# A two-layer hybrid block on one core: seven products of quarters in the feed-forward layer, another order of experts, one weight slot fewer

## The chip, the cores and the metric

The kernel runs on one core of a Trainium2 chip. The metric is the device time of one execution in microseconds (us), lower is better. Engines are named as in the profile: PE (TensorE, matrix products), PEld (its weight loads), DVE (VectorE), ACT (ScalarE), POOL (GpSimd), SP (the queue that issues the transfers).

## The reference

256 tokens of a sequence and 256 tokens of a context, each of width 1024, pass through two layers. The first layer mixes with a gated recurrence and an attention, then applies a dense feed-forward layer to all 512 tokens; the second mixes with a long convolution and a latent attention, then applies eight experts, two of them per token, to the 256 tokens of the sequence. Cut to what the change touches:

```python
D_MODEL, D_FF, N_EXPERTS, TOP_K, D_FF_EXPERT = 1024, 2816, 8, 2, 3584

def swiglu(h, w1, w3, w2):                # all in float32
    return (jax.nn.silu(h @ w1) * (h @ w3)) @ w2

# first layer:  h is 512 x 1024, w1 and w3 are 1024 x 2816, w2 is 2816 x 1024
xl = xl + mod_l[5] * swiglu(modulate(rms_norm(xl, ...)), ffn_w1, ffn_w3, ffn_w2)     # and the same for the context
# second layer: each token goes through its two best experts, with the gates as weights
out = sum(gate * swiglu(t, moe_w1[e], moe_w3[e], moe_w2[e]))
```

## The kernel before, in words

**Products in two parts.** Every float32 matrix is held as a high part (rounded to the engine's fast float32 format, `fp32r`) and a low part (the rest). A product takes three matmuls: high by high, high by low and low by high (`mm3`, L576 to L579). For a weight block, ACT writes the high part (`Stream.split_to`, L260) and DVE the low part, the block minus its high part (`lows`, L273); in some stretches the low part is POOL's (`ws.low = P`).

**Weights.** A `Stream` keeps the list of all weight blocks in the order of their use. A block is 1 MB (128 partitions by 2048 floats). SP loads it into a raw tile, it is split into pairs of tiles `whi` and `wlo` (four of each, 1024 wide) and PE reads these. In the layers before the experts there are two raw tiles.

**The feed-forward layer** (L1093 to L1150). The 22 row tiles (128 wide) of the hidden layer are done in three parts of 8, 8 and 6 (`FFN_PARTS`). In a part, two tiles at a time, which this text calls a pair, PE multiplies a block of w1 (256 columns, eight tiles k of the width) and a block of w3 with the normed input, 48 matmuls of 512 tokens for each block. ACT takes the silu (L1120), DVE multiplies (L1124) and the result is split again (`hilo`, L555 to L557). Then four blocks of w2 finish the part. The first pair of the first part is special: its k loop follows the norm (`norm_pair`, L568: `xn` on DVE L564, `hhi` on ACT L565, `hlo` on DVE L566) and its order is fixed by hand. `tick` (L448) is one small matmul of the modulation vectors; ticks stand between the pairs and the blocks. The tiles `xn` form a ring of four.

**The experts.** Experts are ranked by load: ranks 1 and 2 have room for 128 tokens (full: float32 in two parts, split like above), the other six for 64 (small: plain float32, unsplit). `SEQ` (L345) is the order of the ranks. Each expert is 42 blocks of 1 MB. Blocks flow into a ring of slots (L1475 to L1515), filled in their order as the slots come free (`Stream.fill`, L222); in the last stretch there are 13: five of their own, two raw tiles, five places of buffers that are no longer used, and half of `xT`, the transposed input (L1873), which is free from the middle of the first expert on.

Of the kernel before, what the change touches and what calls it, by code (L numbers as in the profile page):

```python
# [10 lines left out]
F32 = mybir.dt.float32  # L11
# [127 lines left out]
def program(tc, a, out):  # L139
# [174 lines left out]
    for m0, mn in FFN_PARTS:  # L314
        for b in range(mn // 2):
            want(*colblk('ffn_w1', (m0 + 2 * b) * 128, 256))
            want(*colblk('ffn_w3', (m0 + 2 * b) * 128, 256))
        for c0 in range(0, 1024, 256):
            want(*colblk('ffn_w2', c0, 256, m0, m0 + mn))
# [24 lines left out]
    CAP = [64] + [128] * BIG + [64] * (7 - BIG)  # L344
    SEQ = [(x, CAP[x] == 64) for x in (0, 3, 1, 4, 2, 5, 6, 7)]  # L345
    which = {}
# [228 lines left out]

    def mm3(p, wh, wl, xh, xl, first, last):  # L576
        TE.matmul(p, wh, xh, start=first, stop=False)  # L577
        TE.matmul(p, wh, xl, start=False, stop=False)  # L578
        TE.matmul(p, wl, xh, start=False, stop=last)  # L579

# [472 lines left out]
    ap = fx.enter_context(tc.tile_pool(name="ap", bufs=8, reuse_waits="tile"))  # L1053
    mod_ring([(mq, "rm", 2)] * 2 + [(ap, "rm", 6)] * 6, 72)

# [35 lines left out]
    first = [take(0), take(0)]  # L1091
    h = []
    for m0, mn in FFN_PARTS:  # L1093
        act = []
        for b in range(mn // 2):
            if m0 + b == 0:
                p1, p3 = [bank(), bank()], bank2()
                h.append(norm_pair(pb, 0, 1, 0))
                for k in range(KD):
                    if k + 1 < KD:  # L1100
                        h.append(norm_pair(pb, 0, 1, k + 1))
                    for (bh, bl), pq in zip(first, (p1, (p3[:, 0, :], p3[:, 1, :]))):
                        for m in range(2):
                            c = slice(m * 128, m * 128 + 128)
                            mm3(pq[m], bh[:, k, c], bl[:, k, c], h[k][0], h[k][1], k == 0, k == KD - 1)
                ws.split_to(ws.pos[2])
                order.close()
            else:
                bh, bl = take()
                p1 = [bank(), bank()]  # L1110
                for m in range(2):
                    c = slice(m * 128, m * 128 + 128)
                    for k in range(KD):
                        mm3(p1[m], bh[:, k, c], bl[:, k, c], h[k][0], h[k][1], k == 0, k == KD - 1)
                bh, bl = take()
                p3 = bank2()
            for m in range(2):
                c = slice(m * 128, m * 128 + 128)
                s = ap.tile([128, T], F32, name=nm("fs"), tag="fs", bufs=2)
                A.activation(s, p1[m], AF.Silu)  # L1120
                if m0 + b:
                    for k in range(KD):
                        mm3(p3[:, m, :], bh[:, k, c], bl[:, k, c], h[k][0], h[k][1], k == 0, k == KD - 1)
                V.tensor_tensor(s, s, p3[:, m, :], op=OP.mult)  # L1124
                n = len(act) % 4
                if n == 0:
                    ah, al = wide("ah"), wide("al")
                hi, lo = ah[:, n, :], al[:, n, :]
                hilo(hi, lo, s)
                act.append((hi, lo))  # L1130
# [554 lines left out]
    def moe(st, units, slots, main):  # L1685
# [156 lines left out]
        for n in range(len(units) + 1):  # L1842
# [15 lines left out]
            if n:  # L1858
# [52 lines left out]
```

## Time and profile before

| | us |
|---|---|
| runs of before, median of 3 (lowest, highest) | 1726.57 (1723.56, 1729.68) |
| profiled execution, its own time | 1723.7 |
| its span, first to last instruction | 1721.7 |
| PE busy | 1617.6 (94% of the span) |
| DVE busy | 767.6 (45%) |
| ACT busy | 580.3 (34%) |
| POOL busy | 113.0 (7%) |
| bytes moved | 476.03 MB, mean 276 GB/s |

How to read it: the span divides into the first mixing (0 to about 290 us), the feed-forward layer (about 290 to 680), the second mixing (to about 840) and the experts (to the end). The busy share of an engine is a mean over these; what limits a stage is read from that stage. A busy PE is one with matmuls in flight: they are pipelined, so the time of one in the rows is longer than the distance from one start to the next, and it is the distance that counts. The time of DVE and POOL instructions runs from start to end, waiting for memory included.

### The profile page before, as it was taken

How to read it: one execution, taken by the hardware profiler on the slowest of the kernel's cores; microseconds unless marked ns; L12 is line 12 of the kernel's file. 1: busy time of each engine (PE TensorE's matmuls, PEld its weight loads, DVE VectorE, ACT ScalarE, POOL GpSimd, SP SyncE). 2: the span in 40 equal slices, each digit the busy share in tenths (PEclk: the TensorE clock that was granted, in tenths of full speed). 3: DMA queues.
4: the chain of work that ended last, by engine and by line, in shares of the span. 5: the costliest groups of instructions: out<-in, count | busy, mean ns of one | idle time of the engine just before them, and what ended most of it. 6: DMA issues, size and time to landing. Idle time of an engine off the chain costs nothing. (4 is left out here: it accounts for less than half of the span.)

```text
span 1721.7 us, 21415 instructions
## 1 busy us (share of the span) xinstructions
PE 1617.6 (94%) x8369; PEld 1025.8 (60%) x8369; DVE 767.6 (45%) x1214; ACT 580.3 (34%) x872; POOL 113.0 (7%) x81
## 2 busy tenths in 40 slices
PE   6898889999999999989999998999999999988886
PEld 2675666887777776776843434776446763423222
DVE  6679856334333326768630103884128852000001
ACT  3465743322222223554420103674136751000000
POOL 1433200000000000340000000000000000000000
PEclk9998999999999999999999999999999999999999
DMA  9534325223323333553799999999999989999997
GB/s 353 205 120 169 123 98 190 92 98 122 110 105 117 110 104 132 196 202 111 279 386 417 417 418 419 416 417 377 419 413 421 402 302 416 416 419 419 414 419 294
DMA packets 98989, 476.03 MB, mean 276 GB/s; under 512 B 8560, under 2 KB 34544, under 8 KB 53632
## 3 DMA queue, kind: packets, MB, share of 16 engines
q1 hardware_dynamic: 96256, 468.25, 69.3%
q0 software_dynamic: 1536, 5.28, 0.9%
q8 instruction: 68, 1.11, 0.3%
q10 hardware_dynamic: 1088, 1.05, 0.2%
q14 instruction: 41, 0.34, 0.1%
HBM read 471.40 MB, written 3.15 MB: 276 GB/s over the span
## 5 line engine op out<-in xcount | busy, mean ns | idle before, releaser
L273 DVE TENSOR_TENSOR wlo<-raw,whi 128x1024 fp32r<-128x1024 f32 (+2 forms) x240 | 282.1, 1209 | 201.4 <-ACT whi L260 193.9
L260 ACT ACTIVATE whi<-raw 128x1024 fp32r<-128x1024 f32 (+2 forms) x271 | 275.1, 1044 | 280.6 <-PE pm L578 115.7
L1736 PE MATMUL pm<-raw,xs 128*64 128x512 f32 (+1 forms) x1336 | 305.4, 551 | 23.2 <-DMA raw<-in_moe_w_dram 22.5
L1736 PEld LDWEIGHTS pm<-raw,xs 128*64 128x64 f32 x1336 | 103.7, 137 | 190.3 <-issue 138.0
L1855 DVE TENSOR_TENSOR es<-es,pm 128x512 f32<-128x512 f32 (+1 forms) x38 | 24.5, 644 | 339.6 <-PE pm L1736 328.5
L1736 PE MATMUL p<-raw,ats 128*64 128x512 f32 x616 | 152.2, 598 | 5.0 <-DMA raw<-in_moe_w_dram 4.3
L273 POOL TENSOR_TENSOR wlo<-raw,whi 128x1024 fp32r<-128x1024 f32 (+1 forms) x31 | 75.7, 2456 | 559.5 <-ACT k L1236 485.7
L1767 ACT ACTIVATE ats<-pm 128x512 f32<-128x512 f32 (+1 forms) x24 | 13.1, 544 | 285.1 <-PE p L1736 249.9
L577 PE MATMUL pm<-hhi,whi 128*128 128x512 f32 x240 | 96.4, 407 | 3.8 <-ACT hhi L565 3.8
L578 PE MATMUL pm<-hlo,whi 128*128 128x512 f32 x240 | 96.9, 404 | 1.0 <-DVE hlo L566 1.0
L1756 PE MATMUL pm<-wlo,xe 128*128 128x512 f32 x224 | 92.6, 414 | 4.0 <-DVE wlo L273 4.0
L579 PE MATMUL pm<-hhi,wlo 128*128 128x512 f32 x240 | 95.8, 400 | 0.0
L1736 PEld LDWEIGHTS p<-raw,ats 128*64 128x64 f32 x616 | 43.6, 136 | 86.8 <-issue 68.4
L1755 PE MATMUL pm<-whi,xe 128*128 128x512 f32 x224 | 88.0, 399 | 3.0 <-ACT whi L260 3.0
L577 PE MATMUL p<-hhi,whi 128*128 128x512 f32 x224 | 89.0, 398 | 1.3 <-ACT hhi L556 0.7
L578 PE MATMUL p<-hlo,whi 128*128 128x512 f32 x224 | 89.1, 398 | 0.0
L579 PE MATMUL p<-hhi,wlo 128*128 128x512 f32 x224 | 88.8, 396 | 0.0
L1848 ACT ACTIVATE es<-pm 128x512 f32<-128x512 f32 (+1 forms) x38 | 21.2, 559 | 156.2 <-PE pm L1736 150.7
L577 PE MATMUL pm<-ah,whi 128*128 128x512 f32 x176 | 70.2, 402 | 0.0
L458 PE MATMUL pm<-rm,sc 128*32 128x256 f32 x768 | 61.7, 408 | 8.8 <-DMA rm<-in_mod_w_dram 7.4
L578 PE MATMUL pm<-al,whi 128*128 128x512 f32 x176 | 69.6, 397 | 0.0
L579 PE MATMUL pm<-ah,wlo 128*128 128x512 f32 x176 | 69.0, 396 | 0.0
(454 smaller groups left out, 2678.6 us busy)
## 6 DMA issues: line engine op xcount, KB each, us to landing
raw<-in_moe_w_dram SPq DMA_DIRECT2D x300, 1024.0 KB, 15.2
rm<-in_mod_w_dram SPq DMA_DIRECT2D x96, 512.0 KB, 4.7
raw<-in_ffn_w_dram SPq DMA_DIRECT2D x30, 1024.0 KB, 4.8
xT<-in_moe_w_dram SPq DMA_DIRECT2D x24, 1024.0 KB, 18.4
raw<-in_ab_w_in_dram SPq DMA_DIRECT2D x7, 1024.0 KB, 6.6
raw<-in_cd_w_in_dram SPq DMA_DIRECT2D x6, 1024.0 KB, 6.5
whi<-in_moe_w_dram SPq DMA_DIRECT2D x12, 512.0 KB, 15.3
raw<-in_ab_w_out_dram SPq DMA_DIRECT2D x4, 1024.0 KB, 4.9
```

Source lines behind the costliest of these rows:

```text
L260: x = A.activation(h, c, AF.Copy)
L273: x = low.tensor_tensor(l, r, h.bitcast(F32), op=OP.subtract)
L458: TE.matmul(mst[2][32 * i:32 * i + 32, :256], sc[:, k, :], r[:, i * 256:(i + 1) * 256], start=k == 0, stop=k == 7)
L577: TE.matmul(p, wh, xh, start=first, stop=False)
L578: TE.matmul(p, wh, xl, start=False, stop=False)
L579: TE.matmul(p, wl, xh, start=False, stop=last)
L1736: TE.matmul(o if len(w.shape) == 2 else o.rearrange("p (a b) -> p a b", b=S), x, w, start=start, stop=stop)
L1755: TE.matmul(p, xh[:, k, :], bh[:, k, :], start=hf == 0 and k == 0, stop=False)
L1756: TE.matmul(p, xh[:, k, :], bl[:, k, :], start=False, stop=False)
L1767: A.activation(at[:, :n], p[:, :n * 128].rearrange("p (i s) -> p i s", i=n), AF.Copy)
L1848: A.activation(s[:, :w], p1[:, :w], AF.Silu)
L1855: V.tensor_tensor(s[:, :w], s[:, :w], p3[:, :w], op=OP.mult)
```

## The change

All blocks of w1 and w3 but the first pair's are computed by Strassen's scheme: the block is cut into four quarters (128 columns by 512 of the width), the input into four (512 of the width by 256 tokens), and seven products of sums of quarters replace eight products of quarters. `quarters` makes five sums of the input once: three into tiles of their own (products 1, 6, 7; adds on POOL), two in place of quarters that are no longer needed (3, 4; adds on DVE); each is split by ACT and DVE. `Sevens.ahead` makes the weight sums (POOL, for five of the seven) and splits each of the seven (ACT, DVE); `Sevens.block` runs the products (84 matmuls of 256 tokens for a block), and combines them: two copies on ACT, one add on POOL, five adds on DVE. The ring of modulation rows in the feed-forward pool shrinks (`RM`), the order of the experts changes in one place and the slot in `xT` is gone.

```diff
+    RM, SW = 2, 3
-    SEQ = [(x, CAP[x] == 64) for x in (0, 3, 1, 4, 2, 5, 6, 7)]
+    SEQ = [(x, CAP[x] == 64) for x in (0, 3, 1, 4, 5, 2, 6, 7)]
-    mod_ring([(mq, "rm", 2)] * 2 + [(ap, "rm", 6)] * 6, 72)
+    mod_ring([(mq, "rm", 2)] * 2 + [(ap, "rm", RM)] * RM, 72)
...
+    def quarters():
+        for q in (1, 6, 7):
+            sums_q[q] = [ap.tile([128, 4, S], F32R, name=f"h{q}_{t}", tag=f"h{q}{t}", bufs=1) for t in ("hi", "lo")]
+        for k in range(4):
+            x, y = h[k], h[k + 4]
+            for q, (u, cu), (v, cv), op, E in ((1, (x, U0), (y, U1), OP.add, P), (6, (x, U0), (x, U1), OP.add, P),
+                                               (3, (x, U1), (y, U1), OP.subtract, V), (7, (y, U0), (y, U1), OP.add, P),
+                                               (4, (y, U0), (x, U0), OP.subtract, V)):
+                z = nw.tile([128, S], F32, name=nm("xn"), tag="xn", bufs=4)
+                E.tensor_tensor(z, u[0][:, cu].bitcast(F32), v[0][:, cv].bitcast(F32), op=op)
+                E.tensor_tensor(z, z, u[1][:, cu].bitcast(F32), op=OP.add)
+                E.tensor_tensor(z, z, v[1][:, cv].bitcast(F32), op=op)
+                hi, lo = [x[:, k, :] for x in sums_q[q]] if q in sums_q else [x[:, cu] for x in u]
+                A.activation(hi, z, AF.Copy)
+                V.tensor_tensor(lo, z, hi.bitcast(F32), op=OP.subtract)
+    MS = [(5, OP.add, (0, 0), (0, 1)), (2, OP.add, (1, 0), (1, 1)), (1, OP.add, (0, 0), (1, 1)), (3, None, (0, 0), None),
+          (4, None, (1, 1), None), (6, OP.subtract, (1, 0), (0, 0)), (7, OP.subtract, (0, 1), (1, 1))]
...
+        def ahead(self, n):
+            while len(self.parts) < min(n, len(self.todo)):
...
+                if n0 % 2 == 0:
+                    self.t = [wp.tile([128, W // 2], F32R, name=nm(t), tag=t, bufs=2 * NH) for t in ("whi", "wlo")]
...
+                if op:
+                    z2 = ap.tile([128, 4, 128], F32, name=nm("sw"), tag="sw", bufs=SW)
+                    P.tensor_tensor(z2, z, self.r[:, 4 * y[1]:4 * y[1] + 4, 128 * y[0]:128 * y[0] + 128], op=op)
+                    z = z2
+                A.activation(hi, z, AF.Copy)
+                V.tensor_tensor(lo, z, hi.bitcast(F32), op=OP.subtract)
...
+        def block(self, j):
...
+            for i, (q, *_) in enumerate(MS):
+                n0 = 7 * j + i
+                self.ahead(n0 + 5)
...
+                for k in range(4):
+                    mm3(dest[q], hi[:, k, :], lo[:, k, :], *met(q, k), k == 0 and q not in (3, 4, 7), k == 3, q in (3, 4, 7))
+                if q == 5:
+                    A.activation(d, pX, AF.Copy)
+                if q == 2:
+                    A.activation(s2, pY, AF.Copy)
+                    P.tensor_tensor(d, d, s2, op=OP.add)
+                if q == 1:
+                    V.tensor_tensor(t, pZ, d, op=OP.subtract)
+                if q == 6:
+                    V.tensor_tensor(t, t, pW, op=OP.add)
+                    V.tensor_tensor(t, t, pX, op=OP.add)
+            V.tensor_tensor(e, pZ, d, op=OP.subtract)
+            V.tensor_tensor(e, e, pY, op=OP.add)
+            return [[e, pX], [pY, t]]
...
+                j = 2 * (b - (m0 == 0))
+                fs = [ap.tile([128, T], F32, name=nm("fs"), tag="fs", bufs=2) for _ in range(2)]
+                for m, x in enumerate(sevens.block(j)):
+                    for c, u in zip(x, (U0, U1)):
+                        A.activation(fs[m][:, u], c, AF.Silu)
+                for m, x in enumerate(sevens.block(j + 1)):
+                    for c, u in zip(x, (U0, U1)):
+                        V.tensor_tensor(fs[m][:, u], fs[m][:, u], c, op=OP.mult)
+                    activations(fs[m])
...
+            if b == 3 and m0 < 16:
+                sevens = Sevens(FFN_PARTS[m0 // 8 + 1][1])
+                sevens.ahead(4)
...
-                        ws.slots.insert(0, [lambda: xT[:, :, S:], -1, None])
-                        ws.fill()
```

What stands on the engines at the two places of which the prediction speaks:

POOL around the feed-forward layer, before: the last instructions of the first mixing (`hlo`, `u`, `hhi`) are followed at once by those of the second (`wlo` from `raw`); in the feed-forward layer POOL has none.

```order
L885 TENSOR_TENSOR hlo_1854<-u,hhi_1853 128x512
L885 TENSOR_TENSOR hlo_1887<-u,hhi_1886 128x512
L885 TENSOR_TENSOR hlo_1952<-u,hhi_1951 128x512
L273 TENSOR_TENSOR wlo_5169<-raw_5043,whi_5167 128x1024
L273 TENSOR_TENSOR wlo_5170<-raw_5043,whi_5168 128x1024
L273 TENSOR_TENSOR wlo_5260<-raw_5175,whi_5258 128x768
```

POOL at the start of the Strassen pairs, of the change: `sw` are weight sums from a raw block, `xn` the sums of the input's quarters (`hhi`, `hlo`).

```order
L1148 TENSOR_TENSOR sw_2900<-raw_2376 128x512
L1110 TENSOR_TENSOR xn_2679<-hhi_2478 128x256
L1111 TENSOR_TENSOR xn_2673<-xn_2673,hlo_2479 128x256
L1110 TENSOR_TENSOR xn_2691<-hhi_2554 128x256
L1111 TENSOR_TENSOR xn_2679<-xn_2679,hlo_2479 128x256
L1112 TENSOR_TENSOR xn_2673<-xn_2673,hlo_2555 128x256
L1111 TENSOR_TENSOR xn_2691<-xn_2691,hlo_2555 128x256
L1112 TENSOR_TENSOR xn_2679<-xn_2679,hlo_2479 128x256
L1112 TENSOR_TENSOR xn_2691<-xn_2691,hlo_2555 128x256
L1110 TENSOR_TENSOR xn_2703<-hhi_2488,hhi_2576 128x256
```

POOL now has 156 instructions between those two places: 100 weight sums, 36 adds for the input and 20 adds `dd`.

DVE in one pair of the first part, before: low parts of weight blocks (`wlo`, 1024 wide), products with w3's result (`fs`), low parts of the activations (`al`).

```order
L273 TENSOR_TENSOR wlo_2888<-raw_2759,whi_2886 128x1024
L273 TENSOR_TENSOR wlo_2889<-raw_2759,whi_2887 128x1024
L1124 TENSOR_TENSOR fs_2897<-fs_2897,p_508_2896 128x512
L557 TENSOR_TENSOR al_2925<-fs_2897,ah_2924 128x512
L273 TENSOR_TENSOR wlo_2965<-raw_2834,whi_2963 128x1024
L1124 TENSOR_TENSOR fs_2928<-fs_2928,p_508_2896 128x512
L273 TENSOR_TENSOR wlo_2966<-raw_2834,whi_2964 128x1024
L557 TENSOR_TENSOR al_2925<-fs_2928,ah_2924 128x512
```

DVE in the change, between the first and the second Strassen pair: `wlo` is now 512 wide and comes from a weight sum `sw` or from a raw block; `dd` are the combinations, with one input in PSUM (`pm`, `p`).

```order
L1151 TENSOR_TENSOR wlo_3146<-sw_3147,whi_3145 128x512
L1225 TENSOR_TENSOR fs_2818<-fs_2818,dd_2961 128x256
L1151 TENSOR_TENSOR wlo_3146<-sw_3166,whi_3145 128x512
L1225 TENSOR_TENSOR fs_2817<-fs_2817,dd_2962 128x256
L559 TENSOR_TENSOR al_2659<-fs_2818,ah_2658 128x512
L559 TENSOR_TENSOR al_2659<-fs_2817,ah_2658 128x512
L1151 TENSOR_TENSOR wlo_3183<-sw_3184,whi_3182 128x512
L1151 TENSOR_TENSOR wlo_3183<-sw_3200,whi_3182 128x512
L1176 TENSOR_TENSOR dd_3108<-pm_3104,dd_3106 128x256
L1178 TENSOR_TENSOR dd_3108<-dd_3108,pm_3105 128x256
```

Four low parts of 1024 in a pair have become fourteen of 512, and ten combinations have come in. On PE, all the ticks that stood between the pairs and the w2 blocks of the feed-forward layer stand in the first two Strassen pairs.

## Rows read from the trace of the kernel before

**Rows 1.** The page: the span and the number of instructions.

```profile
span 1721.7 us, 21415 instructions
```

**Rows 2.** Busy time by window: us, PE, PEld, DVE, ACT, POOL, PEclk, DMA, GB/s.

```profile
320.00:340.00 20.00, 20.00 (x88) 16.05 (x87) 4.15 (x5) 3.83 (x5) 0.00 (x0) 1.00 0.24 91
640.00:660.00 20.00, 20.00 (x92) 15.36 (x91) 9.88 (x20) 8.98 (x13) 0.00 (x0) 1.00 0.29 93
```

**Rows 3.** Timeline of PE in the feed-forward layer: start us, us, instruction.

```profile
316.80 0.39 PE L577 MATMUL pm<-hhi,whi 128*128 128x512 f32 x1
...
349.83 0.39 PE L577 MATMUL pm<-hhi,whi 128*128 128x512 f32 x1
...
353.34 0.40 PE L577 MATMUL p<-hhi,whi 128*128 128x512 f32 x1
...
668.69 0.64 PE L458 MATMUL pm<-rm,sc 128*32 128x256 f32 x8
669.26 0.50 PE L577 MATMUL pm<-ah,whi 128*128 128x512 f32 x1
...
677.56 0.39 PE L579 MATMUL pm<-ah,wlo 128*128 128x512 f32 x1
```

**Rows 4.** Timeline of PE in the second mixing, 256 tokens wide.

```profile
836.06 0.28 PE L577 MATMUL pm<-hl,whi 128*128 128x256 f32 x1
...
837.12 0.28 PE L577 MATMUL pm<-hl,whi 128*128 128x256 f32 x1
```

**Rows 5.** Timeline of POOL, 143 to 151 us.

```profile
144.31 1.29 POOL L882 TENSOR_TENSOR u<-u,gate 128x512 f32<-128x512 f32 x1 [2.02 <-DVE nr L507]
145.55 2.35 POOL L273 TENSOR_TENSOR wlo<-raw,whi 128x1024 fp32r<-128x1024 f32 x1
147.86 2.26 POOL L882 TENSOR_TENSOR u<-u,gate 128x512 f32<-128x512 f32 x1
```

**Rows 6.** Timeline of DVE in the same stretch and, last, at 157 us.

```profile
144.37 1.23 DVE L783 TENSOR_TENSOR t<-p,nr 128x1024 f32<-128x1024 f32 x1
145.63 3.36 DVE L785 TENSOR_TENSOR t<-t,row 128x1024 f32<-128x1024 f32 x1
149.02 1.25 DVE L793 TENSOR_TENSOR t<-t,rope 128x128 f32<-128x128 f32 x1
150.20 0.28 DVE L794 TENSOR_TENSOR t<-t,rope 128x128 f32<-128x128 f32 x1
...
157.03 1.22 DVE L785 TENSOR_TENSOR t<-t,row 128x1024 f32<-128x1024 f32 x1
```

**Rows 7.** Timeline of DVE at the start of the feed-forward layer.

```profile
290.44 0.48 DVE L566 SCALAR_TENSOR_TENSOR hlo<-xn,modc,hhi 128x256 fp32r<-128x256 f32 x1 [0.18 <-ACT hhi L565]
...
302.31 0.88 DVE L566 SCALAR_TENSOR_TENSOR hlo<-xn,modc,hhi 128x256 fp32r<-128x256 f32 x2 [0.18 <-ACT hhi L565]
...
319.03 1.29 DVE L557 TENSOR_TENSOR al<-fs,ah 128x512 fp32r<-128x512 f32 x2
```

**Rows 8.** Groups by line and shape: count, busy us, mean ns of one, idle before.

```profile
L557 DVE TENSOR_TENSOR al<-fs,ah 128x512 fp32r<-128x512 f32 x22 | 15.1, 689 | 7.2 <-ACT ah L556 7.1
```

**Rows 9.** Busy time by window among the experts, columns as in rows 2.

```profile
1100.00:1120.00 20.00, 20.00 (x86) 15.37 (x85) 17.24 (x17) 14.47 (x17) 0.00 (x0) 1.00 1.02 416
...
1180.00:1200.00 20.00, 20.00 (x90) 9.05 (x90) 3.77 (x4) 7.60 (x10) 0.00 (x0) 1.00 0.84 322
...
1360.00:1380.00 20.00, 20.00 (x89) 16.00 (x88) 16.48 (x16) 15.10 (x17) 0.00 (x0) 1.00 0.96 377
1380.00:1400.00 20.00, 20.00 (x100) 16.12 (x100) 16.97 (x16) 13.32 (x15) 0.00 (x0) 1.00 0.96 357
1400.00:1420.00 20.00, 20.00 (x92) 11.39 (x93) 6.53 (x8) 6.24 (x9) 0.00 (x0) 1.00 0.66 239
```

**Rows 10.** PE's waits, 1000:1080 then 1500:1600: us in total, times, longest.

```profile
PE pm L1736 <- DMA raw<-in_moe_w_dram: 1.0, 2, 0.6
...
PE pm L1736 <- DMA raw<-in_moe_w_dram: 7.7, 9, 1.4
```

**Rows 11.** The page's DMA issues: line, count, KB each, us to landing.

```profile
xT<-in_moe_w_dram SPq DMA_DIRECT2D x24, 1024.0 KB, 18.4
```

**Rows 12.** Busy time by window in the second mixing, columns as in rows 2.

```profile
680.00:700.00 20.00, 17.31 (x134) 12.88 (x127) 18.06 (x43) 9.05 (x19) 0.00 (x0) 0.83 0.26 82
```

More of the change, by code (lines that the diff above doesn't have):

```diff
@@ L315, in program @@
         for b in range(mn // 2):
-            want(*colblk('ffn_w1', (m0 + 2 * b) * 128, 256))
-            want(*colblk('ffn_w3', (m0 + 2 * b) * 128, 256))
+            for w in ('ffn_w1', 'ffn_w3'):
+                src, cols, _, shape = colblk(w, (m0 + 2 * b) * 128, 256)
+                want(src, cols, m0 + b == 0, shape)
         for c0 in range(0, 1024, 256):
@@ L574, in norm_pair, with mm3 @@
         return hi, lo
[L576 to L579, printed above, removed]
+    def mm3(p, wh, wl, xh, xl, first, last, more=False):
+        TE.matmul(p, wh, xh, start=first, stop=False, skip_group_check=more)
+        TE.matmul(p, wh, xl, start=False, stop=False, skip_group_check=more)
+        TE.matmul(p, wl, xh, start=False, stop=last, skip_group_check=more)
     def norm_full():
@@ L1092, in program @@
     h = []
+    U0, U1 = slice(0, S), slice(S, T)
+    sums_q = {}
+    def quarters():
[13 more added lines that the diff above has]
+                V.tensor_tensor(lo, z, hi.bitcast(F32), op=OP.subtract)
@@ L1093, in program, with activations @@
+    sevens = None
     for m0, mn in FFN_PARTS:
         act = []
+        def activations(s):
+            n = len(act) % 4
+            if n == 0:
+                whole[:] = wide("ah"), wide("al")
+            hi, lo = [x[:, n, :] for x in whole]
+            hilo(hi, lo, s)
+            act.append((hi, lo))
+        whole = []
         for b in range(mn // 2):
@@ L1105, in program @@
                             mm3(pq[m], bh[:, k, c], bl[:, k, c], h[k][0], h[k][1], k == 0, k == KD - 1)
-                ws.split_to(ws.pos[2])
                 order.close()
-            else:
[L1109 to L1130, printed above, removed]
+                for m in range(2):
+                    s = ap.tile([128, T], F32, name=nm("fs"), tag="fs", bufs=2)
+                    A.activation(s, p1[m], AF.Silu)
+                    V.tensor_tensor(s, s, p3[:, m, :], op=OP.mult)
+                    activations(s)
@@ new lines, in program @@
+                sevens = Sevens(mn - 2)
+                quarters()
+                sevens.ahead(4)
+            else:
+                j = 2 * (b - (m0 == 0))
[7 more added lines that the diff above has]
+                    activations(fs[m])
@@ L1131, in program @@
             tick()
         for b in range(4):
-            bh, bl = take()
+            bh, bl = take(0 if b == 3 and m0 < 16 else None)
+            if b == 3 and m0 < 16:
+                sevens = Sevens(FFN_PARTS[m0 // 8 + 1][1])
+                sevens.ahead(4)
             for m in range(2):
```

27 lines of the change are left out of this document (added).

## The prediction

> **What bounds the kernel now.** I read the span [rows 1], the busy times by window, and then the timeline of each engine where the change puts work. From 316.80 us, where the pair after the special first one begins, to 677.56 us the feed-forward layer runs on PE alone: PE is busy in all 20 us of a window, DVE in 4 to 10, POOL in none [rows 2]. Starts of 512-token matmuls lie 3.51 us apart over 15 of them, 0.234 us each [rows 3]. So a pair (two blocks of 48) takes 22.5 us. Ten such pairs are 225 us, the w2 blocks 22 x 8 x 3 matmuls or 123.6 us, together 348.6 of the 360.8 us; the remaining 12.2 us fit the ticks, 0.57 us each from one start to the next instruction [rows 3]. Every microsecond PE saves here reaches the end, since all later stages follow from this one, if another resource does not take its place.
>
> Among the experts the bound is the transfer of the weights, 416 GB/s [rows 9], but for three places where all slots are full and the queue waits: 322 GB/s after the first full expert, 377, 357 and 239 during and after the second.
>
> **PE's gain.** A 256-token matmul starts 1.06 us after the ninth before it, 0.118 us each [rows 4], so half the width costs half the time. A block becomes 84 x 0.118 = 9.9 us, a pair 19.8 us: 2.7 us saved, 27 us over ten pairs. That is the whole good of the scheme, and it needs PE to be fed at that pace.
>
> **What feeds it.** POOL's rows and DVE's have to be read together. At 145.55 us POOL starts a 1024-wide subtraction of two tiles in SBUF; DVE's L785, also two tiles in SBUF, starts at 145.63 and takes 3.36 us, where the same line takes 1.22 us at 157.03. It ends at 148.99. POOL's next instruction, 512 wide, takes 2.26 us instead of the 1.29 of the same line before it, ending at 150.12; and DVE's L793 takes 1.25 us, to 0.15 us after that, where its neighbour takes 0.28 [rows 5, 6]. L783, whose input `p` is in PSUM, runs beside POOL in 1.23 us. So a DVE instruction with two inputs in SBUF and a POOL instruction take turns, one waiting for the whole of the other. The Trainium skill (SBUF — State Buffer, Who interferes with whom) has this as a rule: the second SBUF input of DVE comes through the read interface that GpSimd uses, and whoever starts first holds it for the whole instruction. By that rule the adds that the change gives to POOL are not free next to DVE's low parts, and the trace agrees.
>
> So in a Strassen pair the times of POOL and of DVE's two-input instructions add up. POOL: 512 wide 1.24 us (145.55 - 144.31), 1024 wide 2.31 us (147.86 - 145.55) [rows 5]; for 256 wide no row stands, bounds are half of the 512, 0.62, and the 512 itself, 1.24; I take the line through the two known points, 0.70. DVE: 512 wide 1.29 - 0.69 = 0.60 us for each further one, 256 wide 0.88 - 0.48 = 0.40 us [rows 7, 8]. A pair has ten weight sums (12.4) and two `dd` adds (1.4) on POOL, 13.8 us; on DVE fourteen low parts (8.4), two products of `fs` with a `dd` in SBUF (0.8) and two `al` (1.2), 10.4 us. Together **24.2 us**, against 19.8 on PE and the 22.5 (23.1 with its tick) that the pair took before. The ten `dd` combinations read PSUM and can run beside POOL, so they add nothing. ACT, busy in 4 to 9 of 20 us now [rows 2], copies the same number of weight elements and a few 256-wide tiles more; I cost it at nothing. With turns perfectly packed the pairs win nothing; I assume that 5% of the shared time is lost while one engine waits for ACT or for a tile: 25.5 us. Bounds: none lost, and 10%.
>
> **The start.** The input sums are 36 POOL adds of 256 (25.2 us); on DVE 24 adds and 20 low parts (44 x 0.40 = 17.6 us). They can't begin much before 302.3 us, when `hlo` of k = 6 frees the first tile of the `xn` ring [rows 7]. In the order of the change POOL has beside them, up to the last sum, five weight sums (6.2) and two `dd` (1.4), DVE ten low parts of weights (6.0), two `al` (1.2) and the last five norm instructions (2.0): 32.8 + 26.8 = 59.6 us of turns. PE's work of that pair, 19.8 us and 17 ticks (9.7 us), would be over at 346; the sums are over at 361.9. So the first Strassen pair ends some 20 us late, and the next two follow at the turns' pace: 302.3 + 59.6 + 2 x 24.2 - 1.2 (a sum already counted) = 409.1, plus 2 us for the last products; before it was 316.8 + 3 x 23.1 = 386.1. That is +25 us, and +31 with 5% lost.
>
> **Second and third part.** Four products of the next part are prepared during the last w2 block (three sums and four low parts, 6.1 us), so four pairs take 96.8 - 6.1 + 2 = 92.7 us for 92.3 before, three 68.5 for 69.2: about 0; with 5% lost +5 and +3. The eleven ticks that leave the w2 blocks save 6.3 us. The feed-forward layer as a whole: +25 + 0 - 0 - 6.3 = **+19 us** with no loss, 31 + 5 + 3 - 6.3 = **+33 us** with 5%, and +48 us with 10% by the same sum. I take +33. The transfers are covered: a block of 1 MB per 12 us is far below what the experts' stage moves [rows 9].
>
> **The experts.** The three low windows lose (416 - 322) / 416 x 20 = 4.5 us after the first full expert and 1.9 + 2.8 + 8.5 = 13.2 us at the second [rows 9]. PE is then behind the transfers and the slots fill. Ahead of the first full expert PE waits for weights, so all slots are empty; in the 100 us after the second it doesn't catch up, and waits again for data from 1500 us on [rows 10]. With one small expert between the full ones the second starts with slots still filled; with two it starts as the first did. So the new order should turn 13.2 into 4.5. One slot fewer means each stretch fills one block sooner, 1 MB [rows 11] at 416 GB/s or 2.5 us twice: 2 x (4.5 + 2.5) = 14.0 instead of 17.7, **-3.7 us**. Bounds: -8.7 if the slot costs nothing, +5 if the order gains nothing.
>
> The sum: 1723.7 + 33 - 3.7 = 1753 against the profiled execution. That one lies 2.9 us below the median of the runs (1726.57), so I expect **1756 us** as a median. Own range of this case: 1723.7 + 19 - 8.7 + 2.9 = 1737 to 1723.7 + 48 + 5 + 2.9 = 1780.
>
> **Rivals.**
> - *PE stays the bound.* If the turns cost less than the 24.2 us by 4.4 us or more in a pair (POOL's adds shorter on these shapes, or DVE's low parts let in beside them), pairs take 19.8 us. The sums then end after POOL's 32.8 us alone, at 335, before PE's 346, and all 27 us are gained: 1726.6 - 27 - 3.7 = 1696. For it: PE's 0.118 is measured, nothing else in the stage is near its limit. Against it: three instructions in a row that grow by about as long as the other engine still has to run [rows 5, 6]. Chance 0.16.
> - *The start alone costs.* If turns pack perfectly and POOL uses the w2 stretches better than I count, only the +19 remains, with the full -8.7: 1737, the lower end of the own range; it is part of the forecast.
> - *A starved PE loses its clock as well.* From 680 to 700 us PE is busy 17.31 of 20 us and the granted clock is 0.83 [rows 12]. At its lower level, 1.2 GHz, a pair of 39.6 us would exceed the turns' 25. If the 110 us from 302 to 415 ran at 0.83, PE's own work there, 3 x 19.8 + 10 us and the rest of the first pair, would stretch by a fifth, some 15 us, of which most stays hidden in its waits; 5 to 15 us would be added: 1761 to 1771, or more where it falls in every pair, to 1795. Chance 0.10.
> - *The change of slots doesn't help.* If the second full expert still starts with filled slots, the experts cost +5 instead of -3.7: 1765. Chance 0.05, inside the range.
>
> **How the numbers follow.** A difference of 0.3%, 5 us, is about what a measurement of this kernel can tell from none. Forecast 0.64, clock 0.10, slots 0.05: slower, together with the forecast's edge, 0.79. No change (turns packed better than counted and the experts gaining all) 0.05. PE as the bound 0.16. The range that holds 8 in 10 leaves out the fast rival and the far end of the clock's: 1724 to 1783.
>
> **What would show it.** In the profile of the change: POOL's 512-wide sums well over 1.24 us on average and DVE's low parts well over 0.60, with ends that coincide; PE with idle time before the Strassen matmuls, released by DVE `wlo` and by the `h_lo` and `hlo` sums; the first Strassen pair over only near 365 us and the feed-forward layer ending some 30 us later than 677.6. Among the experts, windows of 320 to 380 GB/s of equal size behind both full ones. It is wrong if PE is busy throughout the Strassen pairs, and wrong in size if POOL and DVE leave gaps in which neither runs.

## The result, and the profile after

The change takes 1743.86 us (median of 4 runs, 1742.80 to 1745.87), the kernel before 1725.07 in the same comparison: a ratio of 1.0105, 95% interval 1.0083 to 1.0126. It is slower, as forecast, but by 18.8 us instead of 29.4. The profiled execution took 1742.8 us, its span 19.2 us longer than before [rows 1]. The page of the change:

```profile
span 1740.9 us, 23605 instructions
...
PE 1610.6 (93%) x9089; PEld 1060.6 (61%) x9089; DVE 935.1 (54%) x1478; ACT 644.3 (37%) x1054; POOL 317.9 (18%) x237
...
q1 hardware_dynamic: 76544, 468.25, 67.9%
```

To place the difference I cut both spans at three instructions: the first matmul by ones of the norm ahead of the feed-forward layer, that of the norm behind it, and SP's issue of the first load into `xT`. Timeline of PE before, at the first norm and where the second and the third part begin:

```profile
283.71 1.02 PE L542 MATMUL p<-sa,ones 128*128 128x256 f32 x4
...
430.45 0.40 PE L577 MATMUL pm<-hhi,whi 128*128 128x512 f32 x1
...
571.56 0.50 PE L577 MATMUL pm<-hhi,whi 128*128 128x512 f32 x1
```

The same in the change (line numbers are 2 to 3 higher; L580 to L582 is `mm3`): the norm, the first Strassen matmuls, the first matmul of w2, the second and third part, and the next norm; between them three waits of one pair.

```profile
283.12 1.03 PE L544 MATMUL p<-sa,ones 128*128 128x256 f32 x4
...
319.06 0.28 PE L580 MATMUL p<-hhi,whi 128*128 128x256 f32 x1
319.18 0.28 PE L581 MATMUL p<-hlo,whi 128*128 128x256 f32 x1
...
414.91 0.39 PE L580 MATMUL pm<-ah,whi 128*128 128x512 f32 x1
...
459.90 0.28 PE L580 MATMUL p<-hhi,whi 128*128 128x256 f32 x1
...
511.70 0.38 PE L582 MATMUL p<-hhi,wlo 128*128 128x256 f32 x1 [0.70 <-DVE wlo L1151]
514.83 0.58 PE L580 MATMUL pm<-h_hi,whi 128*128 128x256 f32 x1 [1.69 <-ACT whi L1150]
536.22 0.39 PE L582 MATMUL p<-hhi,wlo 128*128 128x256 f32 x1 [0.70 <-DVE wlo L1151]
...
597.28 0.28 PE L580 MATMUL p<-hhi,whi 128*128 128x256 f32 x1
...
698.91 1.03 PE L544 MATMUL p<-sa,ones 128*128 128x256 f32 x4
```

| us | before | change | difference | forecast |
|---|---|---|---|---|
| up to the first norm | 283.7 | 283.1 | -0.6 | 0 |
| norm, up to the pair after the special one | 33.1 | 35.9 | +2.8 | 0 |
| first part | 113.7 | 140.8 | +27.2 | +25 to +31 |
| second and third part | 247.3 | 239.0 | -8.3 | +1.7 (with no loss -6 to -7) |
| second mixing, to the load into `xT` | 147.8 | 153.4 | +5.6 | 0 |
| experts, to the end | 896.1 | 888.6 | -7.6 | -3.7 |

**Turns.** 511.70 to 536.22 is one Strassen pair: 24.52 us, where PE's 168 matmuls of 0.118 need 19.8 and the sum of turns was 24.2. Busy time by window (us, PE, PEld, DVE, ACT, POOL, PEclk, DMA, GB/s): first pair, a steady pair, and a stretch of w2.

```profile
340.00:360.00 20.00, 15.75 (x119) 10.27 (x120) 15.92 (x28) 7.96 (x18) 12.96 (x16) 0.74 0.67 236
...
500.00:520.00 20.00, 17.61 (x133) 17.17 (x132) 18.14 (x23) 9.44 (x20) 14.59 (x10) 0.91 0.20 69
...
660.00:680.00 20.00, 20.00 (x109) 17.10 (x109) 13.29 (x25) 7.90 (x15) 0.00 (x0) 1.00 0.34 111
```

Groups by line and shape (columns as in rows 8), of POOL over the whole span: the weight sums.

```profile
L1148 POOL TENSOR_TENSOR sw<-raw 128x512 f32<-128x512 f32 x100 | 155.2, 1567 | 196.1 <-DMA raw<-in_ffn_w_dram 110.0 <-DVE wlo L1151 84.0 <-DVE gm L425 2.0
```

And of DVE from 300 to 700 us: the low parts of sums, the products `fs` with a second input in SBUF, and those with one in PSUM.

```profile
L1151 DVE TENSOR_TENSOR wlo<-sw,whi 128x512 fp32r<-128x512 f32 x97 | 85.6, 912 | 13.2 <-ACT whi L1150 13.2
...
L1225 DVE TENSOR_TENSOR fs<-fs,dd 128x256 f32<-128x256 f32 x20 | 17.9, 896 | 0.0
...
L1225 DVE TENSOR_TENSOR fs<-fs,p 128x256 f32<-128x256 f32 x20 | 7.4, 408 | 0.0
```

A sum takes 1.57 us on average instead of 1.24 [rows 5]. The two `fs` groups are the same line and shape: with both inputs in SBUF 896 ns, with one in PSUM 408. In the 24.52 us of that pair POOL and DVE never stand still together, and for only 1.5 us of it DVE runs with an input in PSUM while POOL is idle. The busy shares hide this: DVE's 18.14 and POOL's 14.59 of 20 us add up to more than the window, because the time in which one waits for the other counts as busy in both.

**The ring and the table.** PE's ticks at the two norms wait for their rows of modulation weights (timeline of PE in the change):

```profile
289.49 0.64 PE L460 MATMUL pm<-rm,sc 128*32 128x256 f32 x8 [1.44 <-DMA rm<-in_mod_w_dram]
293.14 1.08 PE L460 MATMUL pm<-rm,sc 128*32 128x256 f32 x8 [3.02 <-DMA rm<-in_mod_w_dram]
...
705.09 0.64 PE L460 MATMUL pm<-rm,sc 128*32 128x256 f32 x8 [0.69 <-DMA rm<-in_mod_w_dram]
707.65 0.64 PE L460 MATMUL pm<-rm,sc 128*32 128x256 f32 x8 [1.92 <-DMA rm<-in_mod_w_dram]
```

And on ACT the square root's table, which the program loads early so that the norm finds it, slid to the first Strassen pairs, where silu overwrote it; it is loaded again inside the norm (timeline of ACT):

```profile
358.89 1.28 ACT L515 ACT_TABLE_LOAD   x1
366.32 1.28 ACT L1222 ACT_TABLE_LOAD   x1
700.46 1.28 ACT L552 ACT_TABLE_LOAD   x1
```

**The experts.** Windows of the change: a full stretch, the first full expert, the second.

```profile
1100.00:1120.00 20.00, 18.77 (x78) 13.94 (x78) 18.41 (x18) 12.95 (x15) 0.00 (x0) 1.00 1.01 424
...
1180.00:1200.00 20.00, 20.00 (x97) 15.97 (x96) 16.12 (x16) 15.08 (x17) 0.00 (x0) 1.00 0.99 393
1200.00:1220.00 20.00, 20.00 (x95) 12.61 (x96) 8.28 (x10) 6.10 (x9) 0.00 (x0) 1.00 0.67 234
...
1500.00:1520.00 20.00, 20.00 (x87) 15.42 (x86) 17.41 (x17) 14.86 (x16) 0.00 (x0) 1.00 1.00 389
1520.00:1540.00 20.00, 20.00 (x103) 14.43 (x103) 9.07 (x9) 7.94 (x10) 0.00 (x0) 1.00 0.74 272
1540.00:1560.00 20.00, 18.90 (x83) 8.47 (x80) 5.92 (x6) 4.41 (x6) 0.00 (x0) 1.00 0.91 378
```

The two dips are now alike, as forecast, but each is deeper than the first one was before, which lost 4.5 us [rows 9]: (31 + 190) / 424 x 20 = 10.4 us and (35 + 152 + 46) / 424 x 20 = 11.0 us. In return a full stretch runs at 424 GB/s instead of 416: the loads into `xT`, which went in small pieces, are gone (96256 packets before, 76544 now, for the same 468.25 MB).

### The profile page after: what moved, and what is told of

Its sections match the earlier page's. It is cut to its first block, busy times and chain, and to the rows that moved or that the text cites. A ratio compares the mean times of both kernels' runs of the same rounds, so it can differ in the third digit from the quotient of the medians.

```text
span 1740.9 us, 23605 instructions
## 1 busy us (share of the span) xinstructions
PE 1610.6 (93%) x9089; PEld 1060.6 (61%) x9089; DVE 935.1 (54%) x1478; ACT 644.3 (37%) x1054; POOL 317.9 (18%) x237
## 3 DMA queue, kind: packets, MB, share of 16 engines
q1 hardware_dynamic: 76544, 468.25, 67.9%
## 4 chain that ended last, share of the span: by engine, by line
PE 42%; DMA 16%; DVE 2%; ACT 1%; issue 1%; POOL 0%; DVEq 0%; SPq 0%; ACTq 0%; POOLq 0%
DMA raw<-in_moe_w_dram 15%; PE pm L1835 10%; PE p L1835 4%; PE pm L1855 3%; PE pm L1857 3%; PE pm L1854 3%; PE p L581 2%; PE p L580 2%; PE p L582 2%; PE pm L580 2%; PE pm L581 2%; PE pm L582 2%; PE pm L1808 1%; PE p L1506 1%; DVE wlo L274 1%
## 5 line engine op out<-in xcount | busy, mean ns | idle before, releaser
L274 DVE TENSOR_TENSOR wlo<-raw,whi 128x1024 fp32r<-128x1024 f32 (+2 forms) x214 | 251.3, 1215 | 71.0 <-ACT whi L261 69.2
L1148 POOL TENSOR_TENSOR sw<-raw 128x512 f32<-128x512 f32 x100 | 155.2, 1567 | 196.1 <-DMA raw<-in_ffn_w_dram 110.0
L580 PE MATMUL p<-hhi,whi 128*128 128x256 f32 (+1 forms) x384 | 119.3, 311 | 7.7 <-ACT hhi L1114 3.6
L582 PE MATMUL p<-hhi,wlo 128*128 128x256 f32 (+1 forms) x384 | 118.4, 308 | 4.3 <-DVE wlo L1151 4.3
L581 PE MATMUL p<-hlo,whi 128*128 128x256 f32 (+1 forms) x384 | 118.2, 308 | 0.0
L1151 DVE TENSOR_TENSOR wlo<-sw,whi 128x512 fp32r<-128x512 f32 x100 | 88.0, 910 | 13.3 <-ACT whi L1150 13.3
L1150 ACT ACTIVATE whi<-sw 128x512 fp32r<-128x512 f32 x100 | 59.9, 626 | 68.6 <-PE pm L581 28.3
L580 PEld LDWEIGHTS p<-hhi,whi 128*128 128x128 f32 x384 | 75.4, 196 | 13.4 <-ACT hhi L1114 4.6
L582 PEld LDWEIGHTS p<-hhi,wlo 128*128 128x128 f32 x384 | 75.3, 196 | 8.4 <-DVE wlo L1151 5.6
L580 PE MATMUL pm<-h_hi,whi 128*128 128x256 f32 x240 | 69.4, 292 | 9.6 <-ACT whi L1150 9.5
```

The lines of the kernel that those rows point to most:

```text
L274: x = low.tensor_tensor(l, r, h.bitcast(F32), op=OP.subtract)
L580: TE.matmul(p, wh, xh, start=first, stop=False, skip_group_check=more)
L581: TE.matmul(p, wh, xl, start=False, stop=False, skip_group_check=more)
L582: TE.matmul(p, wl, xh, start=False, stop=last, skip_group_check=more)
L1148: P.tensor_tensor(z2, z, self.r[:, 4 * y[1]:4 * y[1] + 4, 128 * y[0]:128 * y[0] + 128], op=op)
L1150: A.activation(hi, z, AF.Copy)
```

## The experiments

Every run was timed beside the kernel before on its chip. The stages of each profiled execution, cut as above (the clock is the mean granted clock within the mixing, from one window over it):

| run | feed-forward with its norm | second mixing (clock) | experts |
|---|---|---|---|
| before | 394.1 | 147.8 (0.97) | 896.1 |
| change | 415.8 | 153.4 (0.96) | 888.6 |
| e1 idle sums | 417.4 | 166.1 (0.90) | 886.7 |
| e2 no sums | 383.4 | 156.5 (0.93) | 883.9 |
| e3 sums on DVE | 393.0 | 160.7 (0.94) | 883.9 |
| e4 experts alone | 394.1 | 150.0 (0.95) | 886.0 |
| e5 late start, POOL | 393.7 | 166.2 (0.91) | 887.1 |
| e6 late start, DVE | 382.3 | 164.2 (0.92) | 886.7 |
| e7 with two repairs | 385.2 | 157.1 (0.92) | 885.1 |
| e8 no slot alone | 394.1 | 148.0 (0.97) | 893.7 |
| e9 ring of four alone | 400.3 | 164.5 (0.92) | 896.6 |
| e10 late start, DVE, ring of eight | 377.6 | 147.5 (0.98) | 887.2 |
| e11 order alone | 394.1 | 148.0 (0.97) | 888.2 |
| e12 change, ring of eight | 410.3 | 157.1 (0.95) | 885.0 |

Each row is one execution. Before, e4, e8 and e11 have the same program up to the experts: their layer agrees to 0.1 us, their mixing to 2.2. The runs of e3 and of e5 spread over 11 us each, and the executions shown of e5 and e6 are the longest of theirs, 4.0 us above the medians. So a few microseconds of difference in a mixing prove nothing.

**e1: sums that nobody reads.**

```diff
                     P.tensor_tensor(z2, z, self.r[:, 4 * y[1]:4 * y[1] + 4, 128 * y[0]:128 * y[0] + 128], op=op)
-                    z = z2
+                    pass
```

> The change, but the high and low parts of the weights are made from the raw quarter itself: POOL still makes the same 100 weight sums, and nothing reads them. So the products are of single quarters of the weights, not of sums. Theory 1, taking turns: POOL's sums and DVE's two-input subtractions still share one way into SBUF, 24.2 us of turns in a pair, so a Strassen pair stays at 24 to 25 us (24.5 in the change) and the whole run at 1735 to 1746 us. Theory 2, the chain: pairs are long because the weights of each product pass POOL, ACT and DVE one after the other and PE waits for that chain. Then, with POOL out of the chain, a pair falls to PE's own 19.8 to 20.5 us, ten pairs give 40 us, and the run takes about 1700 us.

Measured: 1755.57 us, ratio 1.0151 (1.0126 to 1.0177). PE's timeline, at the same place of three successive pairs:

```profile
486.12 0.38 PE L580 MATMUL p<-hhi,whi 128*128 128x256 f32 x1 [1.23 <-DVE fs L1225]
...
510.65 0.39 PE L580 MATMUL p<-hhi,whi 128*128 128x256 f32 x1 [1.25 <-DVE fs L1225]
...
536.22 0.38 PE L580 MATMUL p<-hhi,whi 128*128 128x256 f32 x1 [1.24 <-DVE fs L1225]
```

Pairs of 24.5 and 25.6 us, though POOL is out of the chain: the rival falls. The total lies above the expected 1746 because of the mixing (166.1 us), not of the pairs.

**e2: no sums.**

```diff
-                if op:
+                if False:
```

> The change without the 100 weight sums: the high and low parts come from the raw quarter, and POOL makes only the input sums and the adds of two results. It leaves out that part of the computation. Both theories: DVE needs 14.3 us for a pair (14 low parts of 0.60, ten combinations of 0.34, four products, two low parts of activations), PE 19.8, so PE sets the pair: 19.8 to 20.5 us, ten pairs give 40 to 47 us against the change: 1695 to 1705 us. If pairs stay above 22 us, something other than POOL's sums holds them: the lower granted clock of a PE that was starved (0.91 in the windows of the change), or ACT.

Measured: 1709.56 us, 0.9894 (0.9875 to 0.9913). A steady window:

```profile
480.00:500.00 20.00, 20.00 (x171) 20.00 (x170) 15.69 (x31) 11.73 (x25) 1.79 (x2) 1.00 0.30 106
```

PE is busy throughout. The second part begins and ends here (timeline of PE):

```profile
449.57 0.28 PE L580 MATMUL p<-hhi,whi 128*128 128x256 f32 x1
...
574.23 0.28 PE L580 MATMUL p<-hhi,whi 128*128 128x256 f32 x1
```

That is 124.7 us; less 45.0 for w2 (414.91 to 459.90 in the change) and by four, 19.9 us for a pair: PE's own time, as counted. The same reckoning gives 23.1 for the change, less than the 24.5 of a steady pair, since four products are prepared during the w2 block before. The low parts, the same instructions on the same operands, from 300 to 700 us in e1, then the low parts and the `fs` products with both inputs in SBUF in e2:

```profile
L1151 DVE TENSOR_TENSOR wlo<-raw,whi 128x512 fp32r<-128x512 f32 x136 | 137.7, 1039 | 34.0 <-ACT whi L1150 33.9
...
L1151 DVE TENSOR_TENSOR wlo<-raw,whi 128x512 fp32r<-128x512 f32 x136 | 92.8, 719 | 36.5 <-ACT whi L1150 36.3
L1225 DVE TENSOR_TENSOR fs<-fs,dd 128x256 f32<-128x256 f32 x20 | 8.4, 420 | 0.5
```

They take 719 ns on average instead of 1039, and the `fs` products that took 896 in the change take 420. So e1 and e2 together show that POOL's sums cost DVE and through it PE, whether or not they are used. The total is 5 us above the expected range: the input sums of the start are still there, and the first part takes 449.57 - 318.94 = 130.6 us, where PE's own work is 45.0 + 3 x 19.9 = 104.7 and, by estimate, some 10 for 18 ticks of 0.57 [rows 3].

**e3: all sums on DVE.**

```diff
-                    P.tensor_tensor(z2, z, self.r[:, 4 * y[1]:4 * y[1] + 4, 128 * y[0]:128 * y[0] + 128], op=op)
+                    V.tensor_tensor(z2, z, self.r[:, 4 * y[1]:4 * y[1] + 4, 128 * y[0]:128 * y[0] + 128], op=op)
...
-                    P.tensor_tensor(d, d, s2, op=OP.add)
+                    V.tensor_tensor(d, d, s2, op=OP.add)
```
(and V for P in the list of `quarters`)

> The change with every add that POOL made (weight sums, input sums, adds of two results) on DVE. Theory 1, taking turns: a 512-wide add holds the shared way 0.60 us on DVE instead of 1.24 on POOL. DVE's pair is then 14 + 10 times 0.60, 12 combinations of 0.34 to 0.40, four products and two low parts of activations, 21.3 us, and the first pair's sums are over some 12 us sooner. Pairs of 21.3 to 22 us (24.5 in the change), ten of them 25 to 32 us less, the start 8 to 13 less: 1700 to 1712 us, below the kernel before. Theory 2, the chain: POOL's 1.24 us leave the chain, but DVE's queue gets longer; pairs of 23 to 24.5 us and 1730 to 1745 us.

Measured: 1724.25 us, 0.9975 (0.9959 to 0.9991), 12 us above the range of theory 1. The pairs did what it says: the second part takes 583.10 - 455.34 = 127.8 us, 20.7 for a pair by the reckoning that gives 23.1 for the change. The Trainium skill (GPSIMD Engine Reference, 3.1 Elementwise — side-by-side cycle accounting) gives GpSimd about twice DVE's time for an add of two tensors; here it is 1.24 against 0.60 us [rows 5, 7, 8], and in turns all of it counts. But the start did not get shorter. The last input sum's low part, on DVE in the change, then in e3:

```profile
360.11 1.51 DVE L1115 TENSOR_TENSOR hlo<-xn,hhi 128x256 fp32r<-128x256 f32 x1
...
361.05 0.42 DVE L1115 TENSOR_TENSOR hlo<-xn,hhi 128x256 fp32r<-128x256 f32 x1
```

It ends at 361.6 and 361.5 us. DVE stands still in the middle of the sums, behind a tick's result, and PE behind the tick's row (timeline of DVE in e3):

```profile
351.07 0.24 DVE L475 TENSOR_TENSOR modc<-pm,par 128x8 f32<-128x8 f32 x2 [4.64 <-PE pm L471]
```

On PE:

```profile
343.63 1.08 PE L460 MATMUL pm<-rm,sc 128*32 128x256 f32 x8 [3.00 <-DMA rm<-in_mod_w_dram]
```

By the prediction's prices the adds cost 36 x 0.30 + 5 x 0.64 + 2 x 0.30 = 14.6 us less in turns. Against that, the first input sum starts at 311.6 us instead of 306.7, and DVE waits 4.6 and later 2.8 us for PE: 12.3 us together.

**e5, e6: the first part as before, Strassen in the other two.** The input sums are made a quarter at a time beside the four w2 blocks of the first part.

```diff
-            else:
+            elif m0 == 0:
...
+            else:
-                j = 2 * (b - (m0 == 0))
+                j = 2 * b
...
             bh, bl = take(0 if b == 3 and m0 < 16 else None)
+            if m0 == 0:
+                quarters([b])
```

> The change, but Strassen's scheme is used in the second and third part only; the first part is multiplied as in the kernel before, and the input sums are made during it, on the same engines as in the change (POOL and DVE). Theory 1, the start: some 25 to 29 us of the feed-forward layer are lost where PE stands behind the input sums of the first part. Then the first part takes 114 to 118 us as before (140.8 in the change, with 2.3 more ahead of it), the other two 137 and 102 us as in the change, and the run takes 1715 to 1720 us, below the kernel before by what the experts gained. Rival: the three pairs of the first part are long for the same reason as the others (24.5 us), and the sums hide beside them; then only 6 to 8 us come back: 1735 to 1738 us.

Measured: 1728.27 us, 1.0002 (0.9987 to 1.0018). The feed-forward layer is 22.1 us shorter than in the change, as theory 1 of the start has it; the pairs of the first part alone would give 6 to 8. In the profiled execution the mixing is 12.8 us longer than in the change, and the total missed its range by 8 us.

> The same with all sums on DVE. If start and turns are separate costs, both gains add up: the first part 114 to 116 us, the second and third 128 and 95 us as with all sums on DVE (141 and 106 in the kernel before): the feed-forward layer some 24 us shorter than before, 1698 to 1704 us in all. If they are one and the same cost, the time is that of the better of the two, 1715 us or more.

Measured: 1716.40 us, 0.9929 (0.9910 to 0.9947). The total missed its range by 12 us. The layer is 33.5 us shorter than in the change, so the two costs do add up, but by less than expected: the second part takes 136.1 us instead of the 127.8 of e3. The 13 ticks that stand in its pairs, which e3 had in the first pairs, explain most of that: at 0.57 us each [rows 3] an estimate of 7.4 us. The mixing is 10.8 us longer than in the change.

**e7: two repairs behind e6.**

```diff
-            if m0 == 16 and b == 0:
-                warm_sqrt()
...
+    warm_sqrt()
     pb = norm_last(0, 1, p, pn, (1, 71 - mst[1]))
```
(and `tick(2)` for `tick()` in the pairs of the second part)

> The run before this one with two edits that concern the second mixing: the square root's table is loaded at the head of the last norm, in the hand-written order, and each pair of the second part has two ticks, so that four fewer are left for the norm. Theory: the second mixing is 5.6 us longer in the change because the early load of the table slid forward by 300 us and was overwritten by silu's (0.9 us on the path), and because the ring of modulation rows, four instead of eight, makes the ticks wait 2.6 us for their rows. Then 3 to 5 us come back: 1694 to 1700 us. If the cause is another, this run is within 1.5 us of the run before it.

Measured: 1713.99 us, 0.9932 (0.9912 to 0.9951). That is 14 us above the expected range, and 2.4 us below e6 with intervals that overlap: whether the repairs help is undecided. The mixing is 7.1 us shorter, the layer 2.9 longer.

**e4, e8, e11: the experts' edits in the kernel before.**

```diff
-    SEQ = [(x, CAP[x] == 64) for x in (0, 3, 1, 4, 2, 5, 6, 7)]
+    SEQ = [(x, CAP[x] == 64) for x in (0, 3, 1, 4, 5, 2, 6, 7)]
...
-                        ws.slots.insert(0, [lambda: xT[:, :, S:], -1, None])
-                        ws.fill()
```
(both in e4, the second alone in e8, the first alone in e11)

> The kernel before with the experts' part of the change alone: the order (0, 3, 1, 4, 5, 2, 6, 7) and no slot in the transposed input; the feed-forward layer is the old one. Theory 1: what the experts gained in the change (7.6 us from their first weight issue to the end) comes from these two edits: 1714 to 1720 us against 1725. By the trace the transfers run at 422 to 426 GB/s instead of 417, since the pieces of under 2 KB are gone. Rival: it comes from the stages ahead (the mixing ended 26 us later, with the weights further ahead); then within 2 us of before.

Measured: 1717.19 us, 0.9944 (0.9929 to 0.9959), as theory 1 expects.

> The kernel before without the slot in the transposed input, in the old order of experts. By the prediction's term a slot fewer costs 2 x 2.5 us in the full experts: 1732 us. By the trace of the change the slot's loads in pieces of 1 KB slowed every transfer: 417 GB/s with it, 424 without, some 14 us over 352 MB, less the 5 us: 1714 to 1720 us, and the new order gives the rest of what the two edits together gave (1717).

Measured: 1723.08 us, 0.9983 (0.9974 to 0.9992): a gain, so the prediction's +5 us is wrong, but a smaller one than 5 us. Both expectations had only one half. The transfers run at 424 GB/s, and the dip after the first full expert costs (54 + 168) / 424 x 20 = 10.5 us, where the prediction had 4.5 + 2.5:

```profile
1160.00:1180.00 20.00, 20.00 (x107) 16.73 (x106) 15.15 (x15) 13.08 (x15) 0.00 (x0) 1.00 0.97 370
1180.00:1200.00 20.00, 20.00 (x89) 9.59 (x89) 4.87 (x7) 7.54 (x11) 0.00 (x0) 1.00 0.68 256
```

> The kernel before with the new order of experts alone, the slot in the transposed input kept. By the prediction's term the second full expert then starts with empty slots: 13.2 us of lost transfer become 4.5, -8.7 us: 1717 us. By the two runs on the experts (both edits -0.56%, no slot -0.17%) the order is worth 5 to 8 us: 1718 to 1721 us. Rival: the order helps only because the slot is gone; then within 2 us of before.

Measured: 1716.75 us, 0.9949 (0.9935 to 0.9963). The windows at the first and at the second full expert:

```profile
1180.00:1200.00 20.00, 20.00 (x88) 9.44 (x88) 4.70 (x7) 7.56 (x11) 0.00 (x0) 1.00 0.83 323
...
1500.00:1520.00 20.00, 20.00 (x92) 11.12 (x92) 6.13 (x6) 6.50 (x9) 0.00 (x0) 1.00 0.73 289
```

The loss behind the second is down from 13.2 us to (416 - 289) / 416 x 20 = 6.1, that behind the first is what it was. The order alone gives 9.2 us (0.51%), the removal of the slot on top of it nothing that can be measured.

**e9: the ring of four in the kernel before.**

```diff
-    mod_ring([(mq, "rm", 2)] * 2 + [(ap, "rm", 6)] * 6, 72)
+    mod_ring([(mq, "rm", 2)] * 2 + [(ap, "rm", 2)] * 2, 72)
```

> The kernel before with the one edit that the ring of modulation rows has four buffers instead of eight (two of six stay in the feed-forward layer's pool), as in the change. Theory: the ring is a cost of its own that the prediction left out. The ticks around the two norms then wait for their rows (4.4 us at the first norm and 2.6 us at the second in the change), 2 to 3 us of it on the path at the first, 3 to 6 at the second: 1729 to 1735 us. Rival: the waits of the change come from other things (the sums, the table of the square root); then within 2 us of before.

Measured: 1748.52 us, 1.0132 (1.0113 to 1.0151): this one edit costs 22.6 us, far more than either theory allowed. 6.2 us of it are in the feed-forward layer with its norm, 16.7 in the second mixing. One window over the mixing, of the kernel before (columns as above):

```profile
677.79:825.58 147.79, 134.29 (x937) 104.57 (x935) 114.78 (x247) 75.54 (x160) 38.39 (x26) 0.97 0.44 152
```

Of e9:

```profile
684.87:849.39 164.52, 142.70 (x933) 108.45 (x932) 118.30 (x246) 75.01 (x159) 38.59 (x26) 0.92 0.43 149
```

The matmuls and DVE instructions are the same but for a few that fall across the edges. Some 2 MB more are loaded in it, as much as four rows of 512 KB. PE waits for rows 8.5 us instead of 4.8, and its granted clock is lower: with the two levels of 2.4 and 1.2 GHz the exact means, 0.917 and 0.965, stand for some 27 us at the lower one instead of 10. Even if PE had been busy through all of these 17 us they would cost 8.5, and the longer waits 3.7; some 4.5 of the 16.7 us stay unexplained.

**e10: e6 with a ring of eight around both norms.**

```diff
-    mod_ring([(mq, "rm", 2)] * 2 + [(ap, "rm", RM)] * RM, 72)
+    RING = [(mq, "rm", 2)] * 2 + [(ap, "rm", RM)] * RM
+    EXTRA = [(ap, f"h{q}{t}", 1) for q in (1, 6) for t in ("hi", "lo")]
+    mod_ring(RING + EXTRA, 72)
...
                 order.close()
+                rings[:] = RING
...
             if m0 == 16 and b == 0:
-                warm_sqrt()
+                mod_ring(RING + EXTRA, 72)
...
+    warm_sqrt()
     pb = norm_last(0, 1, p, pn, (1, 71 - mst[1]))
```

> Strassen's scheme in the second and third part with all sums on DVE, and eight buffers in the ring of modulation rows around both norms: the tiles of the input sums serve as four of them while they hold no sums. The square root's table is loaded at the head of the last norm. Theory: the ring costs 2.3 us ahead of the feed-forward layer and up to 16 us in the second mixing (164.2 us from the layer's end to the load into the transposed input, against 147.8 before); with both gone 1716 us become 1698 to 1706. If the second mixing was long for another reason, 1709 to 1715 us.

Measured: 1700.09 us (1698.17 to 1702.21), 0.9854 (0.9839 to 0.9869): within the theory's range, and below both kernels. The layer is 16.5 us shorter than before, the experts 8.9, and the mixing is back at its old length:

```profile
661.37:808.90 147.53, 132.91 (x937) 102.51 (x935) 114.88 (x247) 75.74 (x160) 38.35 (x26) 0.98 0.44 152
```

**e12: the change with a ring of eight around both norms** (the edit of e10 on the change, with the first part's four ticks ahead of `quarters`).

> The change itself, with eight buffers in the ring of modulation rows around both norms (the tiles of the input sums 1 and 6 serve as four of them before the sums are made and after the last use), the first part's four ticks ahead of the sums, and the square root's table loaded at the head of the last norm. Theory: the ring costs the change 2 to 3 us ahead of the feed-forward layer and 5 us in the second mixing; its pairs and its start stay as long as they are, since POOL and DVE set them: 1734 to 1738 us. Rival: the ring is also behind the slow start, since the first two pairs hold 17 ticks that wait for their rows; then another 5 to 15 us come back: 1720 to 1731 us.

Measured: 1737.91 us, 1.0074 (1.0055 to 1.0093). The total is what the theory expects, 6 us below the change, with intervals that just overlap, but not in the places it names: the layer with its norm gained 5.5 us and the mixing got 3.7 longer, although its ticks wait 4.3 us for rows, no more than before. The slow start remains, so the rival falls: the first part takes 455.70 - 317.14 = 138.6 us, 140.8 in the change.

## Why the prediction was right, and where it was off

- **PE's gain.** 319.06 and 319.18 above: 0.12 us a matmul, and pairs of 19.9 us in e2, where 168 x 0.118 is 19.8. As counted.
- **The turns.** Right in cause: e1 keeps the sums without their readers and keeps the pairs, e2 drops them and PE is the bound. "PE stays the bound" is thereby out as a rival. By the rule that the prediction names (the Trainium skill, SBUF — State Buffer, Who interferes with whom) a DVE instruction with at most one input in SBUF does not contend with GpSimd; the trace agrees: 408 ns for the `fs` products with one in PSUM, 896 for those with both in SBUF.
- **The size: "I assume that 5% of the shared time is lost".** This is the term that was mis-sized. A pair takes 24.52 us, 1.3% over the 24.2, not 25.5, and the sign that it named for a wrong size, gaps in which neither engine runs, did not appear. The prediction's own sum gives +19 with no loss and +33 with 5% (redone, 5% gives +32 and 10% gives +46, not +48); the three parts together measured 27.2 - 8.3 = +18.9, the no-loss sum.
- **The start.** The sums were forecast to be over at 361.9 us and were at 361.6; the first part is 27.2 us longer, forecast +25 to +31. e5 shows that it is a matter of place: with the sums beside w2 the layer is 22 us shorter. That the end was met to 0.3 us is partly luck: turns are not all that sets it. Without the weight sums (e2) the input sums end at 350.6 us, so POOL's work does hold them; but e3, with 14.6 us less of turns, ends them at 361.5, with a late first sum and waits behind ticks in place of the turns. What the start would take without the ticks was not tried.
- **The experts.** The term of the order was right (13.2 us to 4.5 forecast; 13.2 to 6.1 and -9.2 us in all, e11). The slot's +5 was wrong in both halves: each dip grew by 5 to 6 us (4.5 and 6.1 in e11, 10.4 and 11.0 in the change) and not by 2.5, and the prediction missed that all other loads run faster without the slot's. Alone, its removal gives 2.8 us (e8); with the order, nothing.
- **The second mixing** was not in the sum at all. The prediction told of the smaller ring and gave it no price. In the change the mixing is 5.6 us longer and the norm ahead of the layer 2.8; in the kernel before the ring alone costs 22.6. The account of the error is then: the layer 14.1 us too high (33 for 18.9), 8.4 us not counted (2.8 and 5.6), the experts 3.9 too dear: a net of about 10 us too high. That it is 10 and not 18 is luck: the term left out went the other way.
- **The clock rival.** In the starved windows of the first pair the granted clock was 0.74 to 0.83, as the rival said, but the first part stayed within the forecast without it, so nothing shows a cost there. It was low in the second mixing as well, of which the rival did not speak.

What stays open: why the mixing's clock is low in one program and not in another. All runs whose second norm has a ring of four lie at 153 to 166 us, those with eight at 147 to 150, but for e12 with 157; so the ring is not the only cause. The change, e1 and e2 have the same code from the second norm on, and take 153.4, 166.1 and 156.5 us. The repairs of e7, e10 and e12 change several things at once, and no run lowers the clock by itself.

## What to carry to other kernels

Before giving adds to POOL, look whether DVE reads two SBUF tiles in the same stretch: if so, add the two times up, and ask whether DVE would not do it in half of POOL's. Sums that all later work needs belong into a stretch in which PE is busy with something else, not in front of their first reader. And price every line of a change, the buffers that it takes away above all: in the kernel before, the smaller ring alone cost 22.6 us, most of the 27 that the new scheme could gain.

## What the runs showed that was not expected

The second mixing is the same 937 matmuls, within a few, in nearly every run, and its length roughly follows their mean granted clock: 0.97 to 0.98 with 147.5 to 148.0 us, 0.95 with 150.0 and 157.1, 0.92 with 157.1 to 164.5, 0.90 and 0.91 with 166. PE's waits for rows do not order the runs: 9.1 us in the change with 153.4, 8.5 in e9 with 164.5, 7.2 in e1 with 166.1, 3.2 in e7 with 157.1. What makes the clock fall more often in some of them is not shown.

The slot's loads slow the whole queue a little: 416 GB/s with the slot in `xT` [rows 9], 424 without (e8). Their small pieces are the likely reason, but no run changed the pieces alone. And an early load of an activation table is only early if nothing lets it slide ahead of the last function that uses another table: here it moved by 300 us, and two loads were added.
